# A hybrid SSD / gated DeltaNet block: decay parameters token-major, the convolution's last product and the gate squares on VectorE, the square-root table loaded first

## The chip, the cores and the metric

The kernel runs on one core of a Trainium2 chip. Its time is the device time of one execution in microseconds (us). Five engines of the core work side by side, each through its own in-order list of instructions: TensorE (PE; its weight loads are listed apart as PEld), VectorE (DVE), ScalarE (ACT), GpSimd (POOL) and SyncE (SP), which issues the transfers. Instructions on different engines are ordered by semaphores alone.

## What is computed

One residual layer with two token mixers in parallel, followed by a feed-forward block. 16 meta tokens stand before the 1024 tokens, so the kernel works on 1040 tokens. What matters here, cut from the reference:

```python
proj = up @ w_in                      # z_s, xbc, dt_raw, qkv, a_raw, b_raw, z_d, gates
xbc = silu(causal_depthwise_conv(xbc, ssd_conv_w) + ssd_conv_b)          # SSD: x, B, C
dt = softplus(dt_raw + ssd_dt_bias);  a_head = -exp(ssd_a_log)           # 32 heads
y_s = ssd_chunked(xh, dt, a_head, ...)             # decay exp(cumsum(dt * a_head))
y_s = group_rms(y_s * silu(z_s), SSD_GROUPS) * ssd_norm_w
qkv = silu(causal_depthwise_conv(qkv, dn_conv_w))                        # DeltaNet: q, k, v
beta = sigmoid(b_raw)
g = -exp(dn_a_log) * softplus(a_raw + dn_dt_bias)                        # 16 heads
o = gated_delta_chunked(q, k, v, g, beta)          # decay exp(cumsum(g))
merged = sum(sigmoid(gates) * (branches @ w_branch)) @ w_out
```

The 32 values dt, the 16 of a_raw and the 16 of b_raw come from one projection tile ("dab", kept in r). From them the softplus, the decay logits and beta are made for 48 heads and 1040 tokens.

## The kernel before, in words

The code is written in a tile framework. Its scheduler puts the instructions of the program in an order on each engine ahead of the run, by priorities and its own costs, and sets the semaphores; buffers come from pools. On the chip each engine takes its list strictly in that order. So an instruction that waits holds up everything behind it on its engine.

The stages, in the order of time:

- **Start**, up to about 113 us. The input is normalised in three parts (`norm0`, with the rsqrt of L184 to L186: a Sqrt on ACT, then a reciprocal on DVE). Then come the projection tiles dab, q0, k0, v0 and v1. Each projection (`dense_u`) splits operands in two parts and runs three products for each of eight slices of the contraction: L141 (high by high), L142 (low by high), L143 (high by the weights' low part, `wlo`, made by DVE at L135). A projection has 48 products of 128x400 and smaller ones for the first part of the tokens. Beside them, L298 to L366 make the decay parameters. Here they are computed channel-major, 48 heads on partitions and 1040 tokens along the rows (`n48`, `s`, `s2`, `pp`: a reciprocal at L308 and a polynomial at L313), then transposed in nine pieces by TensorE (L332, L333) and copied out by ACT (L334 to L336). Two products with a triangle and with ones give the cumulative sums (L339, L343).
- **DeltaNet**, about 113 to 1150 us, eight head groups. `conv_tile` (L368) makes one tile of q, k or v: the raw projection is copied to `raw` (L374), one ACT and three DVE instructions form the four taps (L376, L378), ACT takes the tanh (L379), and the last product (1 + tanh) * out is split in two: DVE does 640 of the 1040 columns (L381), while ACT adds one to the other 400 (L380) and POOL multiplies them (`ptt`, L99). The l2 norm then transposes pieces of q and k on TensorE (L446).
- **SSD**, about 1150 to 1830 us, four groups. Its 24 convolution tiles use the same `conv_tile`. A step of `ssd_chunk` forms a block of decays `Es` (L732 on DVE), which TensorE multiplies with the inputs at once (L746). `ssd_z` gates the result and adds up its squares per group: ACT squares (L768), POOL adds (`ptt`, L99, 24 times).
- **Branch products, output projection and feed-forward**, after 1830 us. The change does not touch them.

ACT has tables of functions; an instruction whose function is not in the loaded table is preceded by ACT_TABLE_LOAD. The names that follow keep the numbers of the lines before the change; lines behind it are two to four higher.

Of the kernel before, what the change touches and what calls it, by code (L numbers as in the profile page):

```python
# [21 lines left out]
NM = 16  # L22
# [70 lines left out]
def body(tc, A):  # L93
# [4 lines left out]
    def ptt(out, a, b, op):  # L98
        pool.tensor_tensor(out, a, b, op=op)  # L99
# [136 lines left out]
    bias = const.tile([128, 1], F32, name="bias")  # L236

    with tc.tile_pool(name="start", bufs=2) as sb:
        x = sb.tile([128, KD, TT], F32, name="x0", bufs=1)
# [47 lines left out]
    with tc.tile_pool(name="dab", bufs=1) as sb:  # L287
# [7 lines left out]
        dve.tensor_copy(selD, s0[:, 32:48])  # L295
        alog = sb.tile([48, 1], F32, name="alog")
        sp.dma_start(alog, A["p_alog"])
        act.activation(alog, alog, AF.Exp)  # L298

        n48 = sb.tile([48, TT], F32, name="n48")  # L300
        s = sb.tile([48, TT], F32, name="s48")
        s2 = sb.tile([48, TT], F32, name="s2")
        pp = sb.tile([48, TT], F32, name="pp")
        r48 = r[0:48]
        dve.scalar_tensor_tensor(n48, r48, -1.0, r48, op0=ALU.mult, op1=ALU.min)
        act.activation(n48, n48, AF.Exp)
        dve.tensor_scalar(s, n48, 2.0, None, op0=ALU.add)
        dve.reciprocal(s, s)  # L308
# [6 lines left out]
        dve.tensor_scalar(pp, pp, 2.0, None, op0=ALU.mult)  # L315
        sps = sb.tile([80, TT], F32, name="sps")
        pool.memset(sps, 0.0)
        dve.scalar_tensor_tensor(sps[0:48], r48, 0.0, pp, op0=ALU.max, op1=ALU.add)
        ga = sb.tile([48, TT], F32, name="ga")
        dve.tensor_scalar(ga, sps[0:48], alog, -1.0, op0=ALU.mult, op1=ALU.mult)  # L320
        nb = sb.tile([128, TT], F32, name="nb")
        act.activation(nb[64:80], r[64:80], AF.Tanh, scale=0.5)
        dve.tensor_scalar(sps[64:80], nb[64:80], 1.0, -0.5, op0=ALU.add, op1=ALU.mult)

        gat = sb.tile([128, 9, 48], F32, name="gat")
        lastb = sb.tile([128, 9, 48], F32, name="lastb")
        for t in (dtb, cum, gat, lastb):
            dve.memset(t[:, 8, :], 0.0)
        for c in range(9):
            c0, L = (NM + 128 * c, 128) if c < 8 else (0, NM)  # L330
            ps = psm("p")
            pe.transpose(ps[0:L, 0:80], sps[:, c0:c0 + L], ident[0:80, 0:80])  # L332
            pe.transpose(ps[0:L, 128:176], ga[:, c0:c0 + L], ident[0:48, 0:48])  # L333
            act.copy(dtb[0:L, c, 0:32], ps[0:L, 0:32])  # L334
            act.copy(dtb[0:L, c, 32:48], ps[0:L, 64:80])
            act.copy(gat[0:L, c, :], ps[0:L, 128:176])  # L336
        for t, l in ((cum, tri), (lastb, ones)):
# [30 lines left out]
    def conv_tile(name, out, raw=None):  # L368
# [10 lines left out]
        act.activation(raw[:, 0:TT], out, AF.Tanh)  # L379
        act.activation(raw[:, 0:400], raw[:, 0:400], AF.Identity, bias=ones[:, 0:1])  # L380
        dve.scalar_tensor_tensor(out[:, 400:TT], raw[:, 400:TT], 1.0, out[:, 400:TT], op0=ALU.add, op1=ALU.mult)  # L381
        ptt(out[:, 0:400], raw[:, 0:400], out[:, 0:400], ALU.mult)
        return out
# [369 lines left out]
    def ssd_z(j):  # L753
# [8 lines left out]
        def evac(hf, t):  # L762
            sp.dma_start(y_dram["s", j][:, 512 * hf:512 * hf + 512], t)
            if j % 4 == 0:
                act.activation(sq[hf], t, AF.Square)
            else:
                q = cv.tile([128, 512], F32, name="zt", bufs=3)
                act.activation(q, t, AF.Square)  # L768
                ptt(sq[hf], sq[hf], q, ALU.add)
        ztile(f"zs{j}", yT, 0.5, evac)  # L770
# [467 lines left out]
```

## Time and profile before

| what | value |
|---|---|
| time, median of 3 runs | 3000.81 us (3000.59, 3000.81, 3009.75) |
| profiled execution: own time | 3007.62 us |
| profiled execution: span from first to last instruction | 3005.8 us |
| granted TensorE clock, mean | 0.984 |
| PE busy | 97% of the span |
| DVE / ACT / POOL busy | 66% / 44% / 10% |

The span is 1.8 us shorter than the profiled execution's own time, and that execution is 6.8 us longer than the median. A busy share is an average over stages; the rows further down show single places.

### The profile page before, as it was taken

To read this page: it belongs to the slowest core of one execution; us is meant where nothing else is said; L and a number is where in the kernel's file an instruction comes from. 1 tells how busy PE (TensorE), PEld (TensorE's weight loads), DVE (VectorE), ACT (ScalarE), POOL (GpSimd) and SP (SyncE) were. 2 spreads that over 40 slices of the span, in tenths; PEclk is the share of its full clock that TensorE was granted. 3 is DMA by queue.
4 is the path that set the end of the run, shared out by engine and by line. 5 is a ranking of instruction groups with operands and counts; after the bars stand their busy time and mean duration, and the time that the engine had idled before them with its cause. 6 is when DMAs were issued, how large, how long until landed. Compare 5 with 4: busy or idle time off the path is not lost.

```text
span 3005.8 us, 43124 instructions
## 1 busy us (share of the span) xinstructions
PE 2916.2 (97%) x16130; PEld 2452.7 (82%) x16130; DVE 1974.6 (66%) x3858; ACT 1324.3 (44%) x3319; POOL 289.3 (10%) x274
## 2 busy tenths in 40 slices
PE   7899999999999999999999999999999899999997
PEld 6788788888888879878888778888877688888886
DVE  8577787876867855776768653464568655555446
ACT  5546466456554544555546543212235233333213
POOL 2200000000000000001010100000000333330000
PEclk9999999999999999999999999999999899999998
DMA  3111111111211211111011115343353222226312
GB/s 105 43 57 37 50 50 35 58 50 29 64 33 47 68 43 54 35 57 56 33 60 36 70 61 172 102 139 110 112 182 105 97 80 84 81 81 226 96 53 74
DMA packets 119177, 227.32 MB, mean 76 GB/s; under 512 B 46984, under 2 KB 53800, under 8 KB 118968
## 3 DMA queue, kind: packets, MB, share of 16 engines
q1 hardware_dynamic: 117240, 222.47, 22.7%
q8 instruction: 127, 2.08, 0.3%
q10 hardware_dynamic: 1728, 2.10, 0.2%
q14 instruction: 82, 0.67, 0.1%
HBM read 175.14 MB, written 49.38 MB: 75 GB/s over the span
## 4 chain that ended last, share of the span: by engine, by line
PE 84%; DVE 9%; ACT 3%; DMA 1%; issue 1%; POOL 1%; SPq 0%; DVEq 0%; ACTq 0%; POOLq 0%
PE psd L142 15%; PE psd L143 15%; PE psd L141 15%; PE pq_p L1000 1%; PE pq_p L1001 1%; PE pq_p L1002 1%; PE ps_p L561 1%; PE ps_o L746 1%; PE pq_psd L1001 1%; PE ps_o L639 1%; PE pq_psd L1002 1%; PE pq_psd L1000 1%; PE ps_a L629 1%; PE ps_a L617 1%; PE ps_o L619 1%
## 5 line engine op out<-in xcount | busy, mean ns | idle before, releaser
L142 PE MATMUL psd<-u_lo,whi 128*128 128x512 f32 (+3 forms) x2136 | 770.8, 361 | 3.4 <-DVE u_lo L150 2.3
L141 PE MATMUL psd<-u_hi,whi 128*128 128x512 f32 (+3 forms) x2136 | 764.9, 358 | 1.6 <-ACT raw L374 1.6
L143 PE MATMUL psd<-u_hi,wlo 128*128 128x512 f32 (+3 forms) x2136 | 758.0, 355 | 4.0 <-DVE wlo L135 4.0
L134 ACT CAST whi<-wraw 128x1024 fp32r<-128x1024 f32 (+2 forms) x197 | 188.0, 955 | 649.1 <-PE psd L142 459.6
L142 PEld LDWEIGHTS psd<-u_lo,whi 128*128 128x128 f32 x2136 | 409.6, 192 | 41.3 <-issue 6.8
L143 PEld LDWEIGHTS psd<-u_hi,wlo 128*128 128x128 f32 x2136 | 406.1, 190 | 36.7 <-DVE wlo L135 4.5
L141 PEld LDWEIGHTS psd<-u_hi,whi 128*128 128x128 f32 x2136 | 405.2, 190 | 37.6 <-issue 4.0
L135 DVE TENSOR_TENSOR wlo<-wraw,whi 128x1024 fp32r<-128x1024 f32 (+2 forms) x197 | 217.8, 1106 | 153.5 <-ACT whi L134 147.4
L143 PE MATMUL psd<-blk,wlo 128*128 128x512 f32 x512 | 199.7, 390 | 1.2 <-DVE wlo L135 1.2
L141 PE MATMUL psd<-blk,whi 128*128 128x512 f32 x512 | 199.4, 390 | 0.0
L142 PE MATMUL psd<-blk,whi 128*128 128x512 f32 x512 | 199.4, 389 | 0.0
L374 ACT COPY raw<-psd 128x256 f32<-128x256 f32 x165 | 73.3, 444 | 93.1 <-PE psd L143 89.5
L143 PEld LDWEIGHTS psd<-blk,wlo 128*128 128x128 f32 x512 | 96.2, 188 | 21.8 <-DVE wlo L135 2.0
L906 DVE TENSOR_TENSOR part<-part,psd 128x512 f32<-128x512 f32 x96 | 65.7, 684 | 72.0 <-PE psd L143 72.0
L142 PEld LDWEIGHTS psd<-blk,whi 128*128 128x128 f32 x512 | 96.2, 188 | 20.1
L141 PEld LDWEIGHTS psd<-blk,whi 128*128 128x128 f32 x512 | 96.2, 188 | 19.8
L984 POOL TENSOR_TENSOR sw<-wraw 128x512 f32<-128x512 f32 x44 | 68.4, 1554 | 352.0 <-DMA wraw<-w_gu 240.5
L700 DVE TENSOR_TENSOR xdt<-ps_z,dtb 128x512 f32<-128x512 f32 (+1 forms) x36 | 24.8, 690 | 105.3 <-PE ps_z L697 105.3
L539 DVE TENSOR_TENSOR X<-X,itmp 66x30 f32<-66x30 f32 (+14 forms) x240 | 85.2, 355 | 5.2
L537 DVE TENSOR_TENSOR itmp<-X 66x30 f32<-66x30 f32 (+14 forms) x240 | 81.6, 340 | 5.8 <-DMA X<-nd 0.4
L99 POOL TENSOR_TENSOR qk<-raw,qk 128x400 f32<-128x400 f32 x16 | 30.4, 1900 | 537.6 <-ACT raw L380 423.3
L421 ACT ACTIVATE Es<-ps_p,cum 128x128 f32<-128x128 f32 x256 | 75.3, 372 | 11.1 <-PE ps_p L418 11.0
(686 smaller groups left out, 6277.7 us busy)
## 6 DMA issues: line engine op xcount, KB each, us to landing
wraw<-w_in SPq DMA_DIRECT2D x105, 512.0 KB, 3.3
wraw<-w_gu SPq DMA_DIRECT2D x48, 512.0 KB, 3.3
wraw<-w_br SPq DMA_DIRECT2D x36, 512.0 KB, 3.4
c<-hc SPq DMA_DIRECT2D x22, 512.0 KB, 2.7
hc<-c SPq DMA_DIRECT2D x22, 512.0 KB, 5.9
wraw<-w_dn SPq DMA_DIRECT2D x40, 256.0 KB, 2.6
g<-zt SPq DMA_DIRECT2D x32, 256.0 KB, 2.1
y_d<-zt SPq DMA_DIRECT2D x32, 256.0 KB, 2.0
```

Source lines behind the costliest of these rows:

```text
L134: act.copy(hi[:, 0:kk], raw[:, 0:kk])
L135: dve.tensor_tensor(lo[:, 0:kk], raw[:, 0:kk], hi[:, 0:kk], op=ALU.subtract)
L141: pe.matmul(ps[:, 0:n], hi[:, wk0 + k], ahi(k), start=(k == 0), stop=False)
L142: pe.matmul(ps[:, 0:n], hi[:, wk0 + k], alo(k), start=False, stop=False)
L143: pe.matmul(ps[:, 0:n], lo[:, wk0 + k], ahi(k), start=False, stop=(k == kk - 1))
L374: dense_u((name, lambda ps, p0, p1: act.copy(raw[:, 3 + p0:3 + p1], ps)))
L421: act.activation(E[0:L, i, 0:L], ps[0:L, 128 * i:128 * i + L], AF.Relu, bias=cum[0:L, c, h0 + h:h0 + h + 1], scale=-1.0)
L537: dve.tensor_tensor(t, X[:, 0:j, j:j + 1].broadcast_to([66, j, m]), X[:, j:j + 1, j + 1:32].broadcast_to([66, j, m]), op=ALU.mult)
L539: dve.tensor_tensor(X[:, 0:j, j + 1:32], X[:, 0:j, j + 1:32], t, op=ALU.add)
L906: dve.tensor_tensor(part[:, m, cs], part[:, m, cs], ps, op=ALU.add)
L984: pool.tensor_tensor(t, x, y, op=op)
L1000: pe.matmul(ps, w[0][:, k], y[0][:, k], start=start and k == 0, stop=False, skip_group_check=not start)
```

## The change

1. `bias` is set to 1 and its square root is taken as the first work of ACT, before the inputs arrive. (`bias` gets its real content by the transfer that stood there before.)
2. The decay parameters are computed token-major. The raw tile r is transposed first, in nine pieces of 80 channels; three ACT copies bring it to `tk`, 128 tokens by nine pieces by 80. The chain on DVE then works on 128x432 (9 pieces of 48 heads). The transposes of the results and 27 ACT copies go. `p_alog` is loaded broadcast to 128 partitions.
3. The convolution's last product is one DVE instruction of 128x1040 for each of the 56 tiles. ACT's L380 and POOL's L99 of 400 columns go.
4. The sum of squares of the gated SSD output is added on DVE, 24 times 128x512.

```diff
@@ -235,6 +235,8 @@
     raw0 = cv.tile([128, TT + 3], F32, name="raw")
     bias = const.tile([128, 1], F32, name="bias")
 
+    dve.memset(bias, 1.0)
+    act.activation(bias, bias, AF.Sqrt)
     with tc.tile_pool(name="start", bufs=2) as sb:
         x = sb.tile([128, KD, TT], F32, name="x0", bufs=1)
         wf = []
@@ -293,17 +295,34 @@
         sp.dma_start(s0, A["c_sel"])
         dve.tensor_copy(selS, s0[:, 0:32])
         dve.tensor_copy(selD, s0[:, 32:48])
-        alog = sb.tile([48, 1], F32, name="alog")
-        sp.dma_start(alog, A["p_alog"])
+        alog = sb.tile([128, 48], F32, name="alog")
+        sp.dma_start(alog, V(A["p_alog"], "h o -> o h").broadcast_to([128, 48]))
         act.activation(alog, alog, AF.Exp)
 
-        n48 = sb.tile([48, TT], F32, name="n48")
-        s = sb.tile([48, TT], F32, name="s48")
-        s2 = sb.tile([48, TT], F32, name="s2")
-        pp = sb.tile([48, TT], F32, name="pp")
-        r48 = r[0:48]
+
+        tk = sb.tile([128, 9, 80], F32, name="tk")
+        lastb = sb.tile([128, 9, 48], F32, name="lastb")
+        for t in (tk, cum, lastb):
+            dve.memset(t[:, 8, :], 0.0)
+        for cc in (range(5), range(5, 9)):
+            ps = psm("p")
+            pv = V(ps[:, 0:480], "p (c h) -> p c h", h=96)[:, :, 0:80]
+            for c in cc:
+                c0, L = (NM + 128 * c, 128) if c < 8 else (0, NM)
+                pe.transpose(pv[0:L, c - cc[0]], r[0:80, c0:c0 + L], ident[0:80, 0:80])
+            n = min(len(cc), 8 - cc[0])
+            act.copy(tk[:, cc[0]:cc[0] + n], pv[:, 0:n])
+            if 8 in cc:
+                act.copy(tk[0:NM, 8], pv[0:NM, 3])
+        n48 = sb.tile([128, 9, 48], F32, name="n48")
+        s = sb.tile([128, 9, 48], F32, name="s48")
+        s2 = sb.tile([128, 9, 48], F32, name="s2")
+        pp = sb.tile([128, 9, 48], F32, name="pp")
+        r48 = tk[:, :, 0:48]
         dve.scalar_tensor_tensor(n48, r48, -1.0, r48, op0=ALU.mult, op1=ALU.min)
         act.activation(n48, n48, AF.Exp)
+        nb = sb.tile([128, 9, 16], F32, name="nb")
+        act.activation(nb, tk[:, :, 64:80], AF.Tanh, scale=0.5)
         dve.tensor_scalar(s, n48, 2.0, None, op0=ALU.add)
         dve.reciprocal(s, s)
         dve.tensor_tensor(s, s, n48, op=ALU.mult)
@@ -313,27 +332,12 @@
             dve.scalar_tensor_tensor(pp, pp, 1.0 / c, s2, op0=ALU.add, op1=ALU.mult)
         dve.scalar_tensor_tensor(pp, pp, 1.0, s, op0=ALU.add, op1=ALU.mult)
         dve.tensor_scalar(pp, pp, 2.0, None, op0=ALU.mult)
-        sps = sb.tile([80, TT], F32, name="sps")
-        pool.memset(sps, 0.0)
-        dve.scalar_tensor_tensor(sps[0:48], r48, 0.0, pp, op0=ALU.max, op1=ALU.add)
-        ga = sb.tile([48, TT], F32, name="ga")
-        dve.tensor_scalar(ga, sps[0:48], alog, -1.0, op0=ALU.mult, op1=ALU.mult)
-        nb = sb.tile([128, TT], F32, name="nb")
-        act.activation(nb[64:80], r[64:80], AF.Tanh, scale=0.5)
-        dve.tensor_scalar(sps[64:80], nb[64:80], 1.0, -0.5, op0=ALU.add, op1=ALU.mult)
-
+        dve.scalar_tensor_tensor(pp, r48, 0.0, pp, op0=ALU.max, op1=ALU.add)
         gat = sb.tile([128, 9, 48], F32, name="gat")
-        lastb = sb.tile([128, 9, 48], F32, name="lastb")
-        for t in (dtb, cum, gat, lastb):
-            dve.memset(t[:, 8, :], 0.0)
-        for c in range(9):
-            c0, L = (NM + 128 * c, 128) if c < 8 else (0, NM)
-            ps = psm("p")
-            pe.transpose(ps[0:L, 0:80], sps[:, c0:c0 + L], ident[0:80, 0:80])
-            pe.transpose(ps[0:L, 128:176], ga[:, c0:c0 + L], ident[0:48, 0:48])
-            act.copy(dtb[0:L, c, 0:32], ps[0:L, 0:32])
-            act.copy(dtb[0:L, c, 32:48], ps[0:L, 64:80])
-            act.copy(gat[0:L, c, :], ps[0:L, 128:176])
+        dve.scalar_tensor_tensor(gat, pp, -1.0, alog.unsqueeze(1).broadcast_to([128, 9, 48]),
+                                 op0=ALU.mult, op1=ALU.mult)
+        act.copy(dtb[:, :, 0:32], pp[:, :, 0:32])
+        dve.tensor_scalar(dtb[:, :, 32:48], nb, 1.0, -0.5, op0=ALU.add, op1=ALU.mult)
         for t, l in ((cum, tri), (lastb, ones)):
             ps = psm("p")
             pe.matmul(ps[:, 0:384], l, gat[:, 0:8, :], start=True, stop=True)
@@ -377,9 +381,7 @@
         for i in (1, 2, 3):
             dve.scalar_tensor_tensor(out, raw[:, i:i + TT], w(i), out, op0=ALU.mult, op1=ALU.add)
         act.activation(raw[:, 0:TT], out, AF.Tanh)
-        act.activation(raw[:, 0:400], raw[:, 0:400], AF.Identity, bias=ones[:, 0:1])
-        dve.scalar_tensor_tensor(out[:, 400:TT], raw[:, 400:TT], 1.0, out[:, 400:TT], op0=ALU.add, op1=ALU.mult)
-        ptt(out[:, 0:400], raw[:, 0:400], out[:, 0:400], ALU.mult)
+        dve.scalar_tensor_tensor(out, raw[:, 0:TT], 1.0, out, op0=ALU.add, op1=ALU.mult)
         return out
 
     def ztile(zname, yT, wcol, evac):
@@ -766,7 +768,7 @@
             else:
                 q = cv.tile([128, 512], F32, name="zt", bufs=3)
                 act.activation(q, t, AF.Square)
-                ptt(sq[hf], sq[hf], q, ALU.add)
+                dve.tensor_tensor(sq[hf], sq[hf], q, op=ALU.add)
         ztile(f"zs{j}", yT, 0.5, evac)
 
     def ssd_norm(g):
```

In the order of DVE at the start, the convolution of q0 (`qk`, L378 for the taps and L381 for the last product) runs among the decay chain (`s_...`, `pp`) and the low parts of the weights (`wlo`). Before:

```order
L309 TENSOR_TENSOR s_541<-s_541,n_540 48x1040
L378 SCALAR_TENSOR_TENSOR qk<-raw,convp,qk 128x1040
L310 TENSOR_TENSOR s_542<-s_541 48x1040
L378 SCALAR_TENSOR_TENSOR qk<-raw,convp,qk 128x1040
L311 TENSOR_SCALAR pp<-s_542 48x1040
L135 TENSOR_TENSOR wlo<-wraw,whi 128x1024
L313 SCALAR_TENSOR_TENSOR pp<-pp,s_542 48x1040
L381 SCALAR_TENSOR_TENSOR qk<-raw,qk 128x640
L313 SCALAR_TENSOR_TENSOR pp<-pp,s_542 48x1040
L378 SCALAR_TENSOR_TENSOR qk<-raw,convp,qk 128x1040
L313 SCALAR_TENSOR_TENSOR pp<-pp,s_542 48x1040
L378 SCALAR_TENSOR_TENSOR qk<-raw,convp,qk 128x1040
```

The same stretch of DVE after the change, where L382 and L384 are the taps and the last product, L327 to L333 the chain:

```order
L327 RECIPROCAL s_562<-s_562 128x432
L382 SCALAR_TENSOR_TENSOR qk<-raw,convp,qk 128x1040
L328 TENSOR_TENSOR s_562<-s_562,n_561 128x432
L382 SCALAR_TENSOR_TENSOR qk<-raw,convp,qk 128x1040
L329 TENSOR_TENSOR s_563<-s_562 128x432
L330 TENSOR_SCALAR pp<-s_563 128x432
L332 SCALAR_TENSOR_TENSOR pp<-pp,s_563 128x432
L384 SCALAR_TENSOR_TENSOR qk<-raw,qk 128x1040
L332 SCALAR_TENSOR_TENSOR pp<-pp,s_563 128x432
L135 TENSOR_TENSOR wlo<-wraw,whi 128x1024
L332 SCALAR_TENSOR_TENSOR pp<-pp,s_563 128x432
L382 SCALAR_TENSOR_TENSOR qk<-raw,convp,qk 128x1040
```

The chain's instructions have 432 columns instead of 1040. One `pp` step (L332) stands ahead of the last product of q0, as before (L313). The `wlo` of v0, which stood ahead of L381, is now made in front of the whole chain, outside this piece; the `wlo` behind L384 is that of v1.

On PE, the transpose of q0 for its norm (L446 before, L448 after) stands among the products of v0. Before:

```order
L141 MATMUL psd<-u_hi,whi 128x384
L142 MATMUL psd<-u_lo,whi 128x384
L143 MATMUL psd<-u_hi,wlo 128x256
L141 MATMUL psd<-u_hi,whi 128x256
L142 MATMUL psd<-u_lo,whi 128x256
L143 MATMUL psd<-u_hi,wlo 128x256
L446 MATMUL ps_z<-ident,qk 128x128
L141 MATMUL psd<-u_hi,whi 128x256
```

After:

```order
L141 MATMUL psd<-u_hi,whi 128x256
L142 MATMUL psd<-u_lo,whi 128x256
L143 MATMUL psd<-u_hi,wlo 128x256
L448 MATMUL ps_z<-ident,qk 128x128
L141 MATMUL psd<-u_hi,whi 128x256
```

Before, k0 ends with 400-column products, and six products of 256 columns and two of 384 stand behind them and ahead of the transpose; after, twelve of 256 columns do, of which this shows the last three. Nine new transposes of r (`L312 MATMUL ps_p<-ident,cacc`) stand ahead of k0, right behind q0.

On PE in a step of `ssd_chunk`, `ps_o<-Es,xdt` is the product that takes `Es`, in two groups of four. Before:

```order
L143 MATMUL psd<-u_hi,wlo 128x384
L141 MATMUL psd<-u_hi,whi 128x384
L142 MATMUL psd<-u_lo,whi 128x384
L143 MATMUL psd<-u_hi,wlo 128x384
L746 MATMUL ps_o<-Es,xdt 64x128 x4
L141 MATMUL psd<-u_hi,whi 128x400
L142 MATMUL psd<-u_lo,whi 128x400
L143 MATMUL psd<-u_hi,wlo 128x400
```

After:

```order
L141 MATMUL psd<-u_hi,whi 128x384
L142 MATMUL psd<-u_lo,whi 128x384
L143 MATMUL psd<-u_hi,wlo 128x384
L141 MATMUL psd<-u_hi,whi 128x400
L142 MATMUL psd<-u_lo,whi 128x400
L143 MATMUL psd<-u_hi,wlo 128x400
L748 MATMUL ps_o<-Es,xdt 64x128 x4
L141 MATMUL psd<-u_hi,whi 128x400
```

The second group now stands behind the first three products of 128x400 of the next part, and not ahead of them.

## Rows read from the trace of the kernel before

**Rows 1.** The page: busy time of each engine, and the chain that ended last.

```profile
PE 2916.2 (97%) x16130; PEld 2452.7 (82%) x16130; DVE 1974.6 (66%) x3858; ACT 1324.3 (44%) x3319; POOL 289.3 (10%) x274
...
PE 84%; DVE 9%; ACT 3%; DMA 1%; issue 1%; POOL 1%; SPq 0%; DVEq 0%; ACTq 0%; POOLq 0%
```

**Rows 2.** Waits of PE: engine, line, releaser: total us, times, longest us.

```profile
PE ps_z L446 <- POOL qk L99: 12.1, 1, 12.1
...
PE ps_o L746 <- DVE Es L732: 7.4, 11, 0.7
...
PE psd L143 <- DVE wlo L135: 5.2, 4, 3.1
...
PE ps_o L746 <- ACT raw L374: 1.9, 3, 0.7
```

**Rows 3.** Stretches: us, busy PE, PEld, DVE, ACT, POOL, granted clock, DMA share, GB/s.

```profile
68.50:89.00 20.50, 6.41 (x27) 6.12 (x28) 14.37 (x14) 2.07 (x3) 13.31 (x2) 0.50 0.16 51
...
703.40:713.60 10.20, 10.20 (x51) 7.94 (x51) 3.50 (x15) 4.18 (x16) 0.11 (x1) 0.50 0.01 2
829.70:843.30 13.60, 13.60 (x63) 10.95 (x64) 4.81 (x17) 5.64 (x24) 0.00 (x0) 0.50 0.00 1
1150.00:1830.00 680.00, 670.29 (x4110) 572.93 (x4109) 457.75 (x731) 355.03 (x786) 57.90 (x70) 1.00 0.15 52
```

**Rows 4.** Timeline of PE, 64 to 84.5: start, us, instruction, idle before.

```profile
66.78 0.44 PE L141 MATMUL psd<-u_hi,whi 128*128 128x384 f32 x1 [1.11 <-ACT raw L374]
...
70.50 0.58 PE L143 MATMUL psd<-u_hi,wlo 128*128 128x256 f32 x1 [3.11 <-DVE wlo L135]
...
83.81 0.48 PE L446 MATMUL ps_z<-ident,qk 128*128 128x128 f32 x1 [12.09 <-POOL qk L99]
```

**Rows 5.** Timeline of DVE, 36 to 130.

```profile
56.21 6.64 DVE L308 RECIPROCAL s<-s 48x1040 f32<-48x1040 f32 x1
62.78 1.19 DVE L378 SCALAR_TENSOR_TENSOR qk<-raw,convp,qk 128x1040 f32<-128x1040 f32 x1
...
70.38 1.22 DVE L313 SCALAR_TENSOR_TENSOR pp<-pp,s 48x1040 f32<-48x1040 f32 x1
71.53 0.81 DVE L381 SCALAR_TENSOR_TENSOR qk<-raw,qk 128x640 f32<-128x640 f32 x1
```

**Rows 6.** Timeline of POOL, 36 to 130.

```profile
70.55 13.21 POOL L99 TENSOR_TENSOR qk<-raw,qk 128x400 f32<-128x400 f32 x1 [20.53 <-ACT raw L380]
```

**Rows 7.** Timeline of ACT, 0 to 36.

```profile
12.25 1.28 ACT L185 ACT_TABLE_LOAD   x1
13.54 0.42 ACT L185 ACTIVATE rs<-rs 128x256 f32<-128x256 f32 x1
```

**Rows 8.** Timeline of PE, 106 to 113: the transposes of the results.

```profile
107.22 0.23 PE L332 MATMUL ps_p<-ident,sps 80*128 80x80 f32 x1
107.38 0.26 PE L333 MATMUL ps_p<-ident,ga 48*128 48x48 f32 x1
```

**Rows 9.** Timeline of DVE in an SSD step, 1222 to 1240.

```profile
1232.18 0.69 DVE L732 TENSOR_TENSOR Es<-Es,cbm 128x512 f32<-128x512 f32 x1
1233.40 0.83 DVE L381 SCALAR_TENSOR_TENSOR Bt<-raw,Bt 128x640 f32<-128x640 f32 x1 [0.53 <-ACT raw L379]
1234.15 1.56 DVE L732 TENSOR_TENSOR Es<-Es,cbm 128x512 f32<-128x512 f32 x1
```

**Rows 10.** Timeline of POOL in the same step.

```profile
1234.12 1.05 POOL L99 TENSOR_TENSOR Bt<-raw,Bt 128x400 f32<-128x400 f32 x1 [12.02 <-ACT raw L380]
```

**Rows 11.** Timeline of PE in the same step.

```profile
1235.86 0.66 PE L746 MATMUL ps_o<-Es,xdt 128*64 128x128 f32 x8 [0.67 <-DVE Es L732]
```

**Rows 12.** Groups of ACT by line and shape.

```profile
L380 ACT ACTIVATE raw<-raw,ones 128x400 f32<-128x400 f32 x56 | 35.1, 628 | 0.7
```

**Rows 13.** Groups of POOL by line and shape.

```profile
L99 POOL TENSOR_TENSOR sqs<-sqs,zt 128x512 f32<-128x512 f32 x24 | 30.9, 1287 | 279.0 <-ACT zt L768 190.6 <-issue 88.4
```

**Rows 14.** A stretch of DeltaNet, columns as in group 3.

```profile
500.00:600.00 100.00, 98.85 (x643) 85.72 (x641) 83.01 (x222) 54.80 (x174) 6.04 (x10) 1.00 0.18 54
```

## The prediction

> **What bounds the kernel now.** I read the page first: PE is busy 97% of the span, and 84% of the chain that ended last is PE's own work [rows 1]. The change takes almost nothing from PE, so it can pay only where PE waits, or where its clock is low. So the second view is PE's waits by releaser. Only four of them touch what is edited: one of 12.1 us for POOL's part of the convolution, 5.2 us for the low parts of the weights, and 7.4 + 1.9 = 9.3 us in front of the SSD product that takes `Es` [rows 2]. The reader should see how small this is: 26.6 us of 3006. Third, the granted clock by stretches: from 68.5 to 89 us it is 0.50 (1.2 GHz) with PE busy for 6.41 us only; two further stretches with PE busy throughout also stand at 0.50, 10.2 and 13.6 us long [rows 3]. The timelines then show how each wait comes about.
>
> At the start, PE waits 1.11, 3.11 and 12.09 us within 18 us [rows 4]. The last one is a chain on other engines: POOL's product of 128x400 runs from 70.55 for 13.21 us [rows 6], where the same form takes 1.05 us in an SSD step [rows 10]. DVE works all that time, from 70.38 on, with polynomial steps and taps of 1.2 us each [rows 5]. The 3.11 us has the same origin further up: a reciprocal of 6.64 us over 1040 columns holds DVE, the taps of q0 and the weights' low part queue behind it, and PE starts late on v0 [rows 4, 5].
>
> In an SSD step, the POOL product starts at 1234.12 and the second `Es` at 1234.15; the first `Es` took 0.69 us, this one 1.56 [rows 9, 10]. It ends at 1235.71, and PE resumes at 1235.86 after 0.67 us without work [rows 11]. The trace puts some of these waits down to ACT's L374, which was long done; 14 of them make the 9.3 us [rows 2].
>
> **The change part by part.**
>
> *Square-root table.* Before, ACT reaches its first Sqrt at 12.25, loads for 1.28 us and starts at 13.54 [rows 7]; PE waits for the norm behind it. With the table loaded at the outset, Sqrt starts when its input does, at about 12.25: −1.3 us, at most; zero if the weights of dab are what PE waits for. I take −1.3. The Trainium skill, "ScalarE: Activation LUTs", section "What ACT_TABLE_LOAD costs", gives about 2.66 us for a switch, of which 1.38 us is a drain. Here the activation starts 0.01 us behind the load [rows 7], so the trace does not agree, and the measurement decides; by the page the term would be −2.7.
>
> *Decay parameters.* The reciprocal of 6.64 us over 1040 columns becomes one over 432: 6.64 × 432/1040 = 2.8 us. Each polynomial step of 1.22 us becomes 0.51 by the same ratio [rows 5]. In front of q0's last product DVE does two narrow steps, a reciprocal, three taps and four narrow ones, and the low part for v0 is ahead of all of these. The chain stood at its reciprocal at 56.21 before [rows 5] and can be there no later now. From there: 2.8, three taps of 1.2, four narrow steps of 0.51 and the last product of 1.24 (below) make 9.7, so q0 is ready at 65.9. PE was at the transpose at 83.81 − 12.09 = 71.7; without 1.11, 3.11 and the 1.3 of the table it is there at 66.2 [rows 4]. So the three waits, 16.3 us, go. What could come in their place: the first of them for the transpose by 0 to 1 us, and the cumulative-sum product, which now stands in front of v1, where it needs the whole chain; by adding up the rows of both orders in the same way I count DVE's finish there within a microsecond of PE's arrival. I add +1.5 for both; the bounds are 0 and +5.3, the latter if one reciprocal of 2.8 us, a tap and a low part (1.2 each) more stand ahead. Nine of 18 transposes go, and the nine that come work on a tile that is long ready; the second of a pair starts 0.16 us behind the first [rows 8], so −1.4. 27 ACT copies go and three come, on an engine that is busy 44% [rows 1]; nothing there. `p_alog` now fills 128 partitions instead of 48 values; ACT's table load and exponential wait for it, and behind them on ACT stand v0's high part, q0's evacuation and the three copies of `tk`. Before, that exponential stood at the same place behind a load from the same queue, so I cost it at nothing; if it lands late, all of these and the chain are late by as much, which the +5.3 has to hold.
>
> *Clock.* PE does 6.41 us of work at 0.50 in the stretch that holds these waits [rows 3]. The clock falls where PE has just waited twice. Without waits I expect full clock (2.4 GHz) there: −3.2, half of 6.41; zero if the fall stays.
>
> Start in sum: −1.3 − 16.3 + 1.5 − 1.4 − 3.2 = −20.7.
>
> *Last product.* One DVE instruction of 128x1040: the taps of the same kind and size take 1.19 us, 640 columns take 0.81 to 0.83 [rows 5, 9]; so +0.4 us for each of 56 tiles, 22 us more on DVE. In return POOL no longer reads beside DVE: the `Es` of 1.56 returns to 0.69. ACT loses 56 × 0.63 = 35.1 us [rows 12], which no PE wait hangs on. In an SSD step the second `Es` then ends 0.87 − 0.4 = 0.47 us earlier; the order also puts three products of 128x400 ahead of the waiting group, which start 0.18 us apart, so 0.55 us more cover. 0.47 + 0.55 is over the 0.67 that is waited: −0.67 × 14 = −9.4. Bounds: −4.7, if the slow-down is not all POOL's, and −9.4. The Trainium skill, "SBUF — State Buffer", section "SBUF: two separate sides", says that GpSimd and a VectorE instruction with two SBUF inputs take one port pair in turn, the other blocked for the whole instruction. The trace agrees: 1.05 us of POOL plus 0.69 gives 1.74 from 1234.12, measured end 1235.71, which is 1.59 [rows 9, 10].
>
> In DeltaNet, DVE is busy 83% of a stretch in which PE is busy 99% [rows 14]. 29 of the 32 tiles there add 29 × 0.4 = 11.6 us to a slack of 17% of some 1040 us, and where POOL's product was beside a DVE operation, up to 0.87 us each comes back. I take zero, with ±8.
>
> *Sum of squares.* 24 additions of 128x512 at 0.69 us [rows 9] on DVE, 16.6 us, for 24 of 1287 ns on POOL [rows 13]. SSD has 680 − 458 = 222 us free on DVE [rows 3], so the work is covered. An addition waits for ACT's square and holds what is queued on DVE behind it, at most the 0.63 us of an ACT operation of nearly that size [rows 12]; PE waits only if `Es` is next. Taken as zero; without cover it would be +16.6.
>
> Total: −20.7 − 9.4 = −30.1. On the profiled execution's own 3007.6 that is 2977.5; that execution is 6.8 us over the median of 3000.8, so against the median 2971.
>
> **The rivals.**
>
> *A smaller wait takes the old ones' place.* The transpose of q0 or the cumulative sum now waits for DVE, the clock falls there as it does now, and the SSD gain is the lower bound. Start: −20.7 + 5.3 − 1.5 + 3.2 = −13.7; SSD −4.7; time 3000.8 − 18.4 = 2982. For it: DVE and PE reach these two places within a microsecond of each other by my count, and the order, not the need, fixes what DVE does first. Against it: every step of the chain is less than half as long.
>
> *The clock also stays up in DeltaNet.* The two stretches at 0.50 [rows 3] hold 23.8 us of full work; at full clock half of it goes: −11.9, to 2959. For it: the order of PE changes in DeltaNet. Against it: PE waits on no edited line around them.
>
> *The start's gain does not reach the end.* PE is merely earlier, and a later wait grows by as much, such as one for transfers; the SSD part alone remains, 2991. Against it: with PE busy 97% [rows 1], there is little for it to wait on.
>
> *VectorE becomes the bound (slower).* The place is DeltaNet and SSD: 53 tiles × 0.4 + 24 × 0.69 = 37.8 us more of DVE work behind the start. If all of it reached PE, and the `Es` waits stayed, the time would be 3000.8 − 20.7 + 37.8 = 3018. For it: DVE at 83% in bursts [rows 14], in a strict order. Against it: 17% is free, and POOL's product slows DVE where it overlaps. It decides when over 55% of 37.8 us reaches PE (20.7), and shows as slower from 78%.
>
> **How the numbers follow.** Within 0.3%, about 9 us, this kernel cannot be told from unchanged. Chances: forecast 0.60 (own range 2962 to 2980), smaller wait 0.21, clock up 0.06, gain lost 0.08, VectorE the bound 0.05. The range of 2956 to 2990 takes in the first three with the ±8 of DeltaNet. Faster holds the first three and some of the fourth: 0.90; same: the rest of the fourth and the weak part of the last, 0.06; slower 0.04.
>
> **What the profile after would show.** First Sqrt right behind its input near 12.3 us, five table loads. PE without a wait above 2 us between 60 and 115, clock 1.00 there, and the step to DeltaNet some 20 us earlier. `Es` at 0.69 both times in a step, and no wait of 0.67 at its product. DVE's mean for the last product near 1.24 us. PE waits on `v`, `zt` or `wlo` no larger than before in DeltaNet. Wrong would make it: PE waiting for the last product or for `gat` by several us, `Es` still slow without POOL, or small new PE waits behind DVE summed over 800 steps.

## The result, and the profile after

The changed kernel takes 2961.8 us (median of 4: 2960.1, 2961.6, 2962.0, 2976.4), against 3000.7 for the kernel before on the same chip: ratio 0.9858, 95% interval 0.984 to 0.9877. It is faster by 39 us. The forecast was 2971 with a range from 2956 to 2990. The direction and the main places were right; the gain is 9 us larger than the sum gave.

From here on the names carry the numbers of each kernel's own lines. Of the changed kernel L384 is the convolution's last product (L381 before), L734 makes `Es` (L732), L748 takes it on PE (L746), L448 is the l2 norm's transpose (L446).

The page of the changed kernel, busy time by engine and the chain that ended last:

```profile
PE 2900.6 (98%) x16121; PEld 2442.0 (83%) x16121; DVE 1971.9 (67%) x3882; ACT 1293.4 (44%) x3240; POOL 184.8 (6%) x193
...
PE 91%; DVE 4%; DMA 2%; issue 1%; ACT 1%; POOL 1%; SPq 0%; DVEq 0%; ACTq 0%; POOLq 0%
```

DVE got some 38 us of new work behind the start and is busy for 2.7 us less in all [rows 1]: the shorter chain and the operations that POOL no longer slows pay for it. DVE's share of the chain that ended last fell from 9% to 4%.

The waits of PE from 60 to 90 us, where three waits of 16.3 us in sum stood before [rows 4]:

```profile
PE ps_z L448 <- DVE qk L384: 0.2, 1, 0.2
```

That is the only one, and the windows show PE idle for 0.04 of 20.50 us, at full clock [rows 3]; the second row is the SSD stage:

```profile
68.50:89.00 20.50, 20.46 (x120) 18.15 (x119) 19.01 (x24) 11.59 (x23) 3.51 (x4) 1.00 0.15 52
1115.00:1795.00 680.00, 679.13 (x4168) 581.96 (x4166) 472.40 (x773) 347.05 (x770) 2.23 (x22) 1.00 0.17 57
```

In 680 us of SSD, PE's idle time falls from 9.7 to 0.9 us, and POOL has only the clearing of three columns left. DVE at the start:

```profile
55.62 1.30 DVE L382 SCALAR_TENSOR_TENSOR qk<-raw,convp,qk 128x1040 f32<-128x1040 f32 x1 [0.55 <-ACT qk L380]
...
57.35 2.85 DVE L327 RECIPROCAL s<-s 128x432 f32<-128x432 f32 x1
60.11 1.21 DVE L382 SCALAR_TENSOR_TENSOR qk<-raw,convp,qk 128x1040 f32<-128x1040 f32 x1
...
64.02 0.61 DVE L332 SCALAR_TENSOR_TENSOR pp<-pp,s 128x432 f32<-128x432 f32 x1
64.54 1.23 DVE L384 SCALAR_TENSOR_TENSOR qk<-raw,qk 128x1040 f32<-128x1040 f32 x1
```

And PE at the same moment:

```profile
65.33 0.28 PE L143 MATMUL psd<-u_hi,wlo 128*128 128x256 f32 x1
65.83 0.33 PE L448 MATMUL ps_z<-ident,qk 128*128 128x128 f32 x1 [0.22 <-DVE qk L384]
```

q0 is ready at 65.77 and PE takes it at 65.83. The forecast had 65.9 and 66.2; before, this took until 83.81 [rows 4]. ACT has its table long before the first Sqrt, which starts at 12.15 without a load [rows 7]:

```profile
0.73 1.28 ACT L239 ACT_TABLE_LOAD   x1 [0.73 <-PEq L1231]
2.03 0.20 ACT L239 ACTIVATE bias<-bias 128x1 f32<-128x1 f32 x1
...
12.15 0.42 ACT L185 ACTIVATE rs<-rs 128x256 f32<-128x256 f32 x1
```

An SSD step on DVE, with both `Es` at 0.68 [rows 9]:

```profile
1196.73 0.68 DVE L734 TENSOR_TENSOR Es<-Es,cbm 128x512 f32<-128x512 f32 x1
1197.97 1.24 DVE L384 SCALAR_TENSOR_TENSOR Bt<-raw,Bt 128x1040 f32<-128x1040 f32 x1 [0.56 <-ACT raw L383]
1199.13 0.68 DVE L734 TENSOR_TENSOR Es<-Es,cbm 128x512 f32<-128x512 f32 x1
```

The groups of DVE, for the prices:

```profile
L734 DVE TENSOR_TENSOR Es<-Es,cbm 128x512 f32<-128x512 f32 x64 | 43.5, 685 | 3.6 <-ACT Es L426 3.3
L384 DVE SCALAR_TENSOR_TENSOR xt<-raw,xt 128x1040 f32<-128x1040 f32 x16 | 19.9, 1242 | 11.5 <-ACT raw L383 11.5
...
L771 DVE TENSOR_TENSOR sqs<-sqs,zt 128x512 f32<-128x512 f32 x24 | 16.6, 692 | 12.0 <-ACT zt L770 12.0
```

**Where the time went.** The waits that a view lists miss what PE loses in pieces. So I summed, over all of PE's instructions of a stage, the time from one start to the next, less the tenth percentile of that time for its form in the kernel before. That is PE's loss, what it loses at low clock included.

What low clock costs can be read from two profiles of the changed kernel (the second is g0_after, below). From one group of L563 products to a later one, with 38 operations of DVE and 40 of ACT in between both times, PE needs 16.39 us where the clock is 1.00 (first row) and 23.76 us where 17.07 us of it are at 0.50 (second and third row):

```profile
796.16:812.55 16.39, 16.39 (x138) 12.96 (x134) 9.13 (x38) 9.82 (x40) 0.00 (x0) 1.00 0.01 2
793.24:817.00 23.76, 23.76 (x137) 18.36 (x133) 9.14 (x38) 10.13 (x40) 0.00 (x0) 0.64 0.01 1
795.83:812.90 17.07, 17.07 (x79) 13.08 (x78) 5.80 (x23) 6.38 (x25) 0.00 (x0) 0.50 0.01 1
```

So a microsecond at 0.50 costs (23.76 − 16.39)/17.07 = 0.43 us there. I take 0.43 for all stretches at 0.50 in DeltaNet; where PE also waits in them, that is too much. In the table the start ends, and DeltaNet proper begins, at the first L594 (by the numbers before); SSD runs from the first L697 to the last L777. "Less clock" is DeltaNet's loss less 0.43 of its time at 0.50.

```text
us                  start             DeltaNet proper            SSD
                 loss  at 0.50    loss  at 0.50  less clock     loss
before           61.8   23.9     258.5   27.3      246.7       123.7
after            37.3    0       249.1   13.7      243.2       110.8
g0_after         37.3    0       253.4   23.9      243.2       110.6
e1_table         60.7   20.5     258.7   27.3      247.0       123.7
e2_token_major   43.5    3.4     261.4   34.1      246.7       123.8
e3_conv_dve      48.4   10.2     258.3   34.1      243.6       113.3
e4_squares_dve   63.3   23.9     252.5   13.7      246.6       121.1
f1_pool_in_ssd   39.5    3.4     248.9   13.7      243.0       121.0
f2_pool_in_dn    41.9    0       267.1   47.8      246.6       110.7
f3_pool_beside_ssd 37.7  0       253.3   23.9      243.1       110.9
f4_dve_twice     38.4    0       286.9   54.6      263.4       110.6
g1_dve_dose      40.2    3.4     282.8   41.0      265.1       110.6
g2_dn_640        37.7    0       247.9   17.1      240.5       110.6
g4_values_act    41.4    3.4     239.9    3.4      238.4       110.6
```

The column "less clock" sorts the kernels: the five with POOL's part of the product in DeltaNet stand at 246.6 to 247.0, the five without it and otherwise alike there at 243.0 to 243.6. That is 3.5 us.

A check that needs no sum over instructions: each execution has its span and its mean granted clock on record. Its time at 0.50 is 2 × (1 − clock) × span; I call the span less 0.43 of that its span without low clock. The changed kernel's four executions have spans from 2958.4 to 2974.7 us and come to 2931.8 to 2933.8 in this way, 2932.7 on average; as g0_after it comes to 2933.2. Other kernels' executions scatter by 0.4 to 2.3 us (standard deviation). In the 20.5 us at 0.50 that the kernel before has at its start PE mostly waits, so it can't be compared with the changed kernel in this way, only with kernels that keep that stretch.

The spans of the two profiles differ by 47.4 us: 24.5 at the start, 9.4 in DeltaNet (3.5 at full clock, 5.9 from less time at 0.50) and 12.9 in SSD, while behind SSD the changed kernel loses 1.3 more. The other 1.9 I put down to PE's nine products fewer and its first product, which starts 0.3 us earlier. The medians differ by 39 only, since the profiled execution of before was 6.8 us over its median and that of the changed kernel 1.7 under. The changed kernel's two profiles have 13.7 and 23.9 us at 0.50 in DeltaNet, in other stretches, from the same code. So low clock there varies between executions, and I count none of it as gain; the stretch of 20.5 us at the start is another matter (below).

### The profile page after: what moved, and what is told of

It is laid out like the page before. It is cut to its first block, busy times and chain, and to the rows that moved or that the text cites. A ratio compares the mean times of both kernels' runs of the same rounds, so it can differ in the third digit from the quotient of the medians.

```text
span 2958.4 us, 42844 instructions
## 1 busy us (share of the span) xinstructions
PE 2900.6 (98%) x16121; PEld 2442.0 (83%) x16121; DVE 1971.9 (67%) x3882; ACT 1293.4 (44%) x3240; POOL 184.8 (6%) x193
## 4 chain that ended last, share of the span: by engine, by line
PE 91%; DVE 4%; DMA 2%; issue 1%; ACT 1%; POOL 1%; SPq 0%; DVEq 0%; ACTq 0%; POOLq 0%
PE psd L142 16%; PE psd L141 16%; PE psd L143 16%; PE pq_p L1002 1%; PE pq_p L1003 1%; PE ps_o L748 1%; PE pq_p L1004 1%; PE ps_p L563 1%; PE pq_psd L1002 1%; PE ps_o L641 1%; PE ps_z L448 1%; PE pq_psd L1003 1%; PE pq_psd L1004 1%; PE ps_a L631 1%; PE ps_b L738 1%
## 5 line engine op out<-in xcount | busy, mean ns | idle before, releaser
L378 ACT COPY raw<-psd 128x256 f32<-128x256 f32 x165 | 73.4, 445 | 81.9 <-PE psd L143 80.1
L379 POOL MEMSET raw<- 128x3 f32 x56 | 6.3, 113 | 1393.0 <-DVE qk L384 537.1
L541 DVE TENSOR_TENSOR X<-X,itmp 66x30 f32<-66x30 f32 (+14 forms) x240 | 78.3, 326 | 5.9
```

What stands on the lines that cost most here:

```text
L378: dense_u((name, lambda ps, p0, p1: act.copy(raw[:, 3 + p0:3 + p1], ps)))
L541: dve.tensor_tensor(X[:, 0:j, j + 1:32], X[:, 0:j, j + 1:32], t, op=ALU.add)
```

## The experiments

Each was timed against the kernel before on the same chip, where that had medians of 3007 to 3010 us; so ratios are compared, not times.

**The parts alone**

e1_table: the kernel before with

```diff
+    dve.memset(bias, 1.0)
+    act.activation(bias, bias, AF.Sqrt)
```

> The kernel before with the square-root table loaded first, nothing else. Theory A (the norm of the first part waits for the load): the first Sqrt starts at about 12.3 us in place of 13.54, and the time falls by 1.3 us, to about 2999.4. Rival (PE waits there for the weights of dab and not for the norm): the Sqrt is earlier and the time does not move, 3000.7. Either way the clock fall at 68.5 us and the waits of 1.1, 3.1 and 12.1 us behind it stay.

Ratio 0.999 (0.9977 to 1.0003): the time alone can't tell 1.3 us from nothing. Without low clock the ten executions are 2.1 us below the 21 of the kernel before (2964.5 against 2966.6, with a scatter of 1.5 and 1.8 for a single one), which speaks for theory A. The profile doesn't show it as theory A had it. Sqrt starts at 13.09 and not at 12.3, since ACT waited for weights first:

```profile
10.42 1.04 ACT L134 CAST whi<-wraw 128x1024 fp32r<-128x1024 f32 x1 [1.88 <-DMA wraw<-w_in]
11.50 1.58 ACT L263 ACTIVATE sq<-x 128x384 f32<-128x384 f32 x3
13.09 0.42 ACT L185 ACTIVATE rs<-rs 128x256 f32<-128x256 f32 x1
```

The first L594 starts at 229.8 in place of 231.1. But the kernel before has 3.4 us at 0.50 from 20.7 us on, which this profile has not, and at 0.43 these are 1.5 us; so the 1.3 us can't be put down to the table.

e2_token_major: the kernel before with the block from `alog` to `dtb` of the change (hunks 2 and 3 of the diff).

> The kernel before with the decay parameters token-major, nothing else; POOL still does 400 columns of each convolution product. Theory A (the long chain on DVE makes the waits at the start; POOL is starved because DVE has no gap): with steps of 0.5 us POOL's product of q0 ends within 3 us, the waits of 1.1, 3.1 and 12.1 us go, the clock stays at 1.00, and the time falls by 17 to 24 us, to 2977 to 2984; the waits of 0.67 us for Es stay. Theory B (POOL beside a busy DVE is the cause by itself): POOL's product of q0 still takes over 6 us, PE still waits over 5 us at the transpose, and the fall is under 12 us.

Ratio 0.9954 (0.9936 to 0.9972), SSD unchanged. POOL's product of q0, and the one wait of PE over 1 us from 60 to 90:

```profile
66.86 1.25 POOL L99 TENSOR_TENSOR qk<-raw,qk 128x400 f32<-128x400 f32 x1 [18.56 <-ACT raw L382]
```

```profile
PE ps_z L448 <- POOL qk L99: 1.3, 1, 1.3
```

The same POOL operation takes 1.25 us in place of 13.21 [rows 6], as theory A expected, but not for its reason: DVE has no gap here either. POOL gets in behind DVE's product, and of the next two steps, of 0.60 us each, one is held:

```profile
66.40 0.82 DVE L383 SCALAR_TENSOR_TENSOR qk<-raw,qk 128x640 f32<-128x640 f32 x1
67.13 2.08 DVE L330 SCALAR_TENSOR_TENSOR pp<-pp,s 128x432 f32<-128x432 f32 x2
```

In the kernel before POOL's product ended at 83.76 [rows 6], 0.9 us behind the last step of DVE's row, which ended at 82.87. Why the row of 1040 columns let nothing in and this one does is not shown. PE's loss at the start falls by 18.3 us, that of the low clock there included; the time, by 14 us, less than the 17 to 24 expected.

e3_conv_dve: the kernel before with

```diff
-        act.activation(raw[:, 0:400], raw[:, 0:400], AF.Identity, bias=ones[:, 0:1])
-        dve.scalar_tensor_tensor(out[:, 400:TT], raw[:, 400:TT], 1.0, out[:, 400:TT], ...)
-        ptt(out[:, 0:400], raw[:, 0:400], out[:, 0:400], ALU.mult)
+        dve.scalar_tensor_tensor(out, raw[:, 0:TT], 1.0, out, op0=ALU.add, op1=ALU.mult)
```

> The kernel before with the convolution's last product in one DVE operation, nothing else. Theory A: in SSD the second Es falls from 1.56 to 0.69 us and 11 to 12 us go there; at the start the wait of 12.1 us shrinks to under 2 us, but the wait for the weights' low part (3.1 us) stays, since the chain of 1040 columns does: in all -20 to -25 us, 2976 to 2981. Theory B (the start's waits belong to the chain of 1040 columns alone): PE still waits over 5 us at the transpose, and only the 12 us of SSD come, 2989. Rival C (VectorE as the bound): 22 us more on DVE reach PE in DeltaNet and SSD, and the time is above 2990 though the wait at the start is gone.

Ratio 0.9909 (0.9878 to 0.9939), 27 us, a little more than theory A expected. PE's waits from 60 to 90 us:

```profile
PE psd L143 <- DVE wlo L135: 3.2, 1, 3.2
PE psd L141 <- ACT raw L374: 1.1, 1, 1.1
```

The wait of 12.1 us is gone with the long chain still in place; the two that belong to that chain stay. PE's loss falls by 13.4 us at the start, by 3.1 in DeltaNet at full clock and by 10.4 in SSD. So the long wait needed both, POOL's product and the row of DVE operations as it was, and either edit removes it. That is why the parts sum to more than the whole: at the start e1, e2 and e3 give 1.1 + 18.3 + 13.4 = 32.8 us against 24.5.

e4_squares_dve: the kernel before with

```diff
-                ptt(sq[hf], sq[hf], q, ALU.add)
+                dve.tensor_tensor(sq[hf], sq[hf], q, op=ALU.add)
```

> The kernel before with the squares of the gated SSD output added on DVE, nothing else. Theory A: the 16.6 us of 24 additions lie in DVE's slack, and the time stays within 2 us of 3000.7. Rival C (VectorE as the bound): up to 16.6 us reach PE, 3010 to 3017, with PE waits for Es or xdt in SSD longer than 0.67 us. Rival D: POOL's additions slowed DVE where they overlapped, and the time falls by 2 to 4 us.

Ratio 0.9989 (0.9976 to 1.0003), unclear by time. In the profile PE loses 2.6 us less in SSD, which is theory D's size. D's mechanism is on DVE's rows: in the kernel before 14 of the 64 `Es` take 1.55 to 1.57 us beside POOL's convolution product, and seven more take 0.90 to 1.76 us beside one of POOL's additions. POOL and, below it, DVE:

```profile
1388.60 1.28 POOL L99 TENSOR_TENSOR sqs<-sqs,zt 128x512 f32<-128x512 f32 x1 [5.85 <-ACT zt L768]
```

```profile
1388.67 1.75 DVE L732 TENSOR_TENSOR Es<-Es,cbm 128x512 f32<-128x512 f32 x1
```

In e4 these seven are at 0.69 us and the other 14 as before; the listed `Es` waits stay too (11 of 7.4 us), so what PE gains lies in pieces that no wait shows. VectorE as the bound is refuted for SSD.

**The changed kernel with something put back or put in**

f1_pool_in_ssd and f2_pool_in_dn: `conv_tile` with

```diff
+        if name[0] in "xBC":        # f2: "qkv"
+            (the three lines of the old split)
+        else:
             dve.scalar_tensor_tensor(out, raw[:, 0:TT], 1.0, out, op0=ALU.add, op1=ALU.mult)
```

> The changed kernel, but with the old split of the convolution's last product (640 columns on DVE, 400 on POOL behind ACT) in the 24 SSD tiles. Theory A (POOL's product in an SSD step slows Es, and PE waits for it): the 14 waits of 0.67 us come back, SSD is 10 to 11 us longer than in the changed kernel, the start and DeltaNet are as in it; ratio to the kernel before 0.989 to 0.9895. Rival (the gain in SSD came from the order of PE or from the squares): SSD is less than 4 us longer.

Ratio 0.9895 (0.9878 to 0.9913); PE loses 10.2 us more in SSD, as theory A has it; start and DeltaNet are within 1 us of the changed kernel's, low clock aside. Without low clock its executions stand at 2944.9, 12 us above the changed kernel. Fourteen waits of 0.7 us are back, and `Es` on DVE reads as before:

```profile
1199.12 0.69 DVE L739 TENSOR_TENSOR Es<-Es,cbm 128x512 f32<-128x512 f32 x1
1200.36 0.82 DVE L386 SCALAR_TENSOR_TENSOR Bt<-raw,Bt 128x640 f32<-128x640 f32 x1 [0.55 <-ACT raw L383]
1201.10 1.56 DVE L739 TENSOR_TENSOR Es<-Es,cbm 128x512 f32<-128x512 f32 x1
```

POOL in the same step:

```profile
1201.06 1.04 POOL L99 TENSOR_TENSOR Bt<-raw,Bt 128x400 f32<-128x400 f32 x1 [12.03 <-ACT raw L385]
```

> The changed kernel, but with the old split of the convolution's last product in the 32 DeltaNet tiles (the first at the start among them). Theory A: start and DeltaNet lose 8 to 13 us outside the stretches at low clock, as the token-major kernel alone stands behind the changed one there; SSD is as in the changed kernel; ratio to before about 0.990. Rival C (the DVE work added in DeltaNet costs about what POOL's slow-downs give back): under 3 us.

Ratio 0.9916 (0.9895 to 0.9937). PE loses 4.6 us more at the start and, at full clock, 3.4 in DeltaNet proper: 8.0, the lower edge of theory A. The spans without low clock agree, 2941.6 against 2932.7. In this profile DeltaNet has 34 us more at 0.50 than in that of the changed kernel, so its span alone says little.

f3_pool_beside_ssd: behind the product in SSD

```diff
+        if name[0] in "xBC":
+            ptt(raw[:, 0:400], raw[:, 400:800], raw[:, 400:800], ALU.mult)
```

> The changed kernel with 24 useless POOL products of 128x400, one behind each convolution product in SSD; its result goes to the raw tile, which nobody reads any more, so the output is unchanged. The orders of PE and DVE are those of the changed kernel. Theory A (POOL's reads hold DVE's next operation with two SBUF inputs): the second Es of a step takes 1.56 us again; it ends 0.4 us later than before the change, PE arrives 0.55 us later, so PE waits about 0.5 us in 14 steps and SSD is 7 us longer. Rival (Es was slow for another reason, the order or ACT's operation): Es stays at 0.69 and the time does not move.

Theory A fails here as I put it: SSD is unchanged (110.9). The ratio, 0.9884 (0.9865 to 0.9903), is no better than f1's, but these executions had more time at 0.50 (83 us on average, f1's 65); without low clock they stand at 2932.7, as the changed kernel does. DVE and, below it, POOL:

```profile
1202.88 1.24 DVE L384 SCALAR_TENSOR_TENSOR Bt<-raw,Bt 128x1040 f32<-128x1040 f32 x1 [0.68 <-ACT raw L383]
1204.04 0.69 DVE L736 TENSOR_TENSOR Es<-Es,cbm 128x512 f32<-128x512 f32 x1
```

```profile
1204.21 1.23 POOL L99 TENSOR_TENSOR raw<-raw 128x400 f32<-128x400 f32 x1 [13.07 <-DVE Bt L384]
```

POOL now waits for the end of DVE's product, and so starts 0.17 us behind `Es`. `Es` is not slowed; POOL is, which takes 0.85 us for the same operation away from `Es`. The 64 `Es` of f1 and, below, of f3:

```profile
L739 DVE TENSOR_TENSOR Es<-Es,cbm 128x512 f32<-128x512 f32 x64 | 55.9, 878 | 3.6 <-ACT Es L431 3.3
L736 DVE TENSOR_TENSOR Es<-Es,cbm 128x512 f32<-128x512 f32 x64 | 43.6, 686 | 3.6 <-ACT Es L428 3.3
```

In f1 and in the kernel before, POOL waits for ACT only, is ready while DVE's product runs, and starts 0.03 to 0.04 us ahead of `Es` [rows 9, 10]. So a POOL product beside DVE isn't what costs; one that is ready first does. The Trainium skill, "SBUF — State Buffer", section "SBUF: two separate sides", says that whichever starts first has the shared ports for the whole instruction; both runs agree with that, 1.56 against 0.69 us. A useless POOL product that is ready early and leaves PE's order alone wasn't tried; f1 moves PE's order too, so how much of the 10.2 us is the order's stays open.

f4_dve_twice and g1_dve_dose add DVE work behind each product:

```diff
+        dve.scalar_tensor_tensor(raw[:, 0:TT], out, 1.0, out, op0=ALU.add, op1=ALU.mult)   # f4
+        dve.tensor_tensor(out, out, out, op=ALU.max)                                       # g1
```

> The changed kernel with the last product of each of the 56 convolution tiles followed by a useless DVE operation of the same size and kind (into the raw tile): 56 x 1.24 = 69 us more on DVE, three times what the change added. Theory A (DVE has slack): under 20 us of it reach PE, most in DeltaNet. Rival C (VectorE is close to being the bound): over 40 us. In between, the forecast of zero for the added DVE work held only because its dose was small.

> The changed kernel with a useless DVE operation of 128x1040 on the finished tile in place (a maximum of the tile with itself) behind each of the 56 products. Unlike the doubled product it does not hold the raw tile. Theory A (in DeltaNet most of what is added to DVE reaches PE): start and DeltaNet lose 25 to 39 us of the 39 added there, SSD nothing of its 29. Rival (the doubled product cost so much since it held the raw tile and ACT's copies waited): under 15 us.

Ratios 0.9948 (0.9931 to 0.9964) and 0.9954 (0.9939 to 0.9969). Low clock aside, PE's loss in start and DeltaNet grows by some 21 and 23 us of the 39 added there, and the spans without low clock say the same (2954.0 and 2956.4, so 21 and 23 above the changed kernel); SSD does not move (110.6 in both). Holding the raw tile was not the cause. So f4 came out between its two theories, near A, and g1 a little under its theory A (25 to 39) and over the rival's 15: SSD has slack, DeltaNet has some for a part of the dose. PE's largest waits in g1 from 40 to 1140 us:

```profile
PE psd L141 <- ACT raw L378: 5.8, 11, 1.3
PE ps_z L673 <- DVE v L664: 4.1, 3, 3.5
PE ps_p L564 <- DVE T L553: 4.0, 1, 4.0
```

g0_after and g2_dn_640, the latter with

```diff
+        c0 = 400 if name[0] in "qkv" else 0
+        dve.scalar_tensor_tensor(out[:, c0:TT], raw[:, c0:TT], 1.0, out[:, c0:TT], ...)
```

> The changed kernel again, as the measure for the three kernels beside it on the same chip. Ratio to the kernel before 0.984 to 0.988 as in the first measurement; outside the stretches at low clock start and DeltaNet together within 1 us of the first profile, and SSD the same.

> The changed kernel with only 640 of 1040 columns of the last product done in the 32 DeltaNet tiles (the other 400 columns are left out, so they lack the factor), on DVE, without POOL and ACT. It is the cost of the widening without the return of POOL's slow-downs. Theory A: 32 x 0.4 = 13 us less on DVE bring 5 to 12 us in start and DeltaNet; so the change gained some 20 us there from POOL and gave up to half of it back. Rival (the widening is free in DVE's slack): under 2 us.

The repeat gave 0.986 (0.9839 to 0.9882), and 37.3, 243.2 and 110.6 us of loss: with low clock taken off, the accounting repeats to 0.2 us. g2, which leaves 400 columns of these tiles without their factor: 0.9827 (0.9809 to 0.9845). At full clock it loses 2.3 us less than the changed kernel for 13 us less on DVE (3.7 by the spans without low clock), between the rival's under 2 and theory A's 5 to 12, and nearer the rival's. By time it is 12 us faster than the repeat beside it. The rest is low clock: its four executions have a mean clock of 0.989 to 0.991, the changed kernel's eight 0.984 to 0.991. So at full clock the widening costs 2 to 4 us.

g4_values_act: the scaling of the value tiles on ACT

```diff
-                dve.tensor_tensor(v[:, 4 * hf:4 * hf + 4, h], V(ps, "p (c k) -> p c k", k=128),
-                                  nirk[:, 4 * hf:4 * hf + 4].unsqueeze(2).broadcast_to([128, 4, 128]),
-                                  op=ALU.mult)
+                for c in range(4):
+                    act.activation(v[:, 4 * hf + c, h], ps[:, 128 * c:128 * c + 128], AF.Identity,
+                                   scale=nirk[:, 4 * hf + c:4 * hf + c + 1])
```

> The changed kernel with the scaling of the transposed value tiles taken from DVE (32 operations of 128x512 from PSUM, 0.69 us each) to ACT (128 of 128x128). If DVE's time in DeltaNet is what PE feels, 22 us less of it bring 5 to 15 us. Rival: the single bank of these transposes comes free later, as four ACT operations take over 0.9 us against 0.69, and PE waits up to 10 us more.

```profile
L488 ACT ACTIVATE v<-ps_z,nirk 128x128 f32<-128x128 f32 x128 | 37.8, 377 | 13.2 <-PE ps_z L486 12.6 <-DVE nirk L462 0.5
```

ACT pays 37.8 us (the group above) for 22 on DVE, and the kernel is the fastest of the study: 0.9818 (0.98 to 0.9836); its four runs, 2950.5 to 2955.9, lie below all four of the changed kernel beside it, 2958.8 to 2971.0. Low clock aside, PE loses 2.2 us less (3.4 by the spans without low clock); the rest of the 14 us is less low clock. That isn't one lucky profile: all four executions have a mean clock of 0.991 or 0.992. With g2, these are the two kernels with less work for DVE in DeltaNet, and both have less time at 0.50 (58 and 50 us on average against 71 and 73). What links the two is not shown.

## Why the prediction was right, step by step

- **Table** (−1.3): Sqrt at 12.15 in place of 13.54. e1's executions support a gain of this size, its profile does not show it.
- **Waits at the start** (−16.3, +1.5 for new ones): right in place and size. One wait of 0.22 us is left. That q0 was ready at 65.77 where 65.9 was forecast is partly luck: the reciprocal started at 57.35 and not by 56.21, and one of the three taps that the sum puts behind it stood ahead of it, at 55.62; the two errors cancel. The story of the 12.1 us was incomplete: e2 and e3 show that either edit alone removes it.
- **Clock** (−3.2): the stretch at 0.50 from 68.5 us is at 1.00 after the change, in e2 too; it is there in e1 (20.5 us) and a little later in e4 (17.1 us), which keep the waits, and for 6.8 us in e3, which keeps two of them. What went with the waits is shown; the rule behind it isn't.
- **Start in sum**: PE loses 24.5 us less where the forecast had 19.3 (20.7 less the 1.4 of the transposes, which are work and not loss). 1.5 of the difference is the short stretch at 0.50 from 20.7 us, which comes and goes among these kernels. The rest no listed wait of the kernel before explains; f2 shows that POOL's part of the product costs 4.6 us at the start even beside the short chain.
- **`Es` in SSD** (−9.4): e3 gives −10.4, f1 +10.2. The mechanism was right; the listed waits (9.3 us) understate it by a tenth.
- **Squares** (0): −2.6 with e4. The forecast asked only what the additions would cost DVE, and missed that on POOL they held `Es` as the convolution's product did. SSD in sum: −10.4 − 2.6 = −13.0, measured −12.9.
- **DeltaNet** (0, ±8): 3.5 us gained at full clock, within the bounds. The cost that the forecast set against the returns, "29 × 0.4 = 11.6 us", is 2 to 4 us by g2; the returns are then some 6 to 7, less than the "up to 0.87 us each" would give for every tile. That the two nearly cancel was assumed, not worked out. The 17% of slack is real for that dose; of the 39 us of g1, 23 reach PE.
- **The 9 us beyond the sum** are so spread over start (5), DeltaNet (3.5), squares (2.6) and `Es` (1), of which the stages behind SSD take back 1.3 and the short stretch at 0.50 is luck. No single term was far off.
- **Rivals**: the smaller wait did not come. The clock did not stay up in DeltaNet: 13.7 and 23.9 us at 0.50 in the two profiles, against 27.3. The gain of the start reached the end: the stages behind SSD lose only 1.3 us more. VectorE is not the bound, but in DeltaNet it is close: g1 stands at 0.9954 where the changed kernel stands at 0.986.

## What to carry to other kernels

A product on POOL that is ready while DVE runs may start ahead of DVE's next operation and hold it, or be held off itself by a row of DVE operations; look at both engines' rows before giving POOL a share of a DVE step. A slack read as a busy share can be good for a small dose and bad for three times as much, so test it with a useless operation of the size in question. When several edits meet at one wait, measure each alone: here two removed the same 12 us. And take low clock off, at a price read from the traces, before comparing kernels by a few microseconds: f1 and f3 have nearly the same ratio and differ by 12 us without it.

## What the runs showed of the hardware

POOL's operation of 128x400 took 13.21 us beside a row of DVE operations without a gap [rows 6], and 1.25 us beside another such row, of narrower steps (e2). A POOL operation that came 0.17 us behind a DVE operation did not slow it, while one that came 0.04 us ahead took it from 0.69 to 1.56 us. Stretches at 0.50 came in DeltaNet while PE had no wait at all, and the same kernel showed them in different places in two executions (10.2 and 3.4 us; 3.4, 17.1 and 3.4 us). A microsecond at 0.50 cost PE 0.43 us there, not half, so the difference between the two is worth some 4.4 us.
